# Feed-forward chunks by 512 weight columns, key-block products by 128 columns, 400 GB/s in the planner

## The chip, the core and the metric

The kernel runs on one NeuronCore of one Trainium2 chip. The metric is the device time of one execution in microseconds (us); lower is better.

## What is computed

Two layers on a sequence of 256 tokens of width 1024, batch 1. Each layer is feed-forward, attention, feed-forward. Every one of the six blocks is normalised and modulated by vectors that come from a conditioning vector `c`, and its result is added through a gate. The attention of layer 0 has 16 query and 4 key heads and a window of 128 tokens; that of layer 1 has 16 heads with forget gates.

```python
c_act = jax.nn.silu(c)
for layer in range(DEPTH):
    mod = (c_act @ ada_w[layer] + ada_b[layer]).reshape(B, 3, 3, D_MODEL)
    h = modulate(x, norm_g[layer, 0], mod[:, 0, 0], mod[:, 0, 1])
    x = x + 0.5 * mod[:, 0, 2][:, None, :] * swiglu(h, ffn_w13[layer, 0], ffn_w2[layer, 0])
    h = modulate(x, norm_g[layer, 1], mod[:, 1, 0], mod[:, 1, 1])
    y = swa_mixer(...) if layer == 0 else fox_mixer(...)
    x = x + mod[:, 1, 2][:, None, :] * y
    h = modulate(x, norm_g[layer, 2], mod[:, 2, 0], mod[:, 2, 1])
    x = x + 0.5 * mod[:, 2, 2][:, None, :] * swiglu(h, ffn_w13[layer, 1], ffn_w2[layer, 1])

def swiglu(h, w13, w2):
    gate, up = jnp.split(h @ w13, 2, axis=-1)
    return (jax.nn.silu(gate) * up) @ w2
```

The inner width of the feed-forward is 2816. All inputs are float32.

## The kernel before

**Precision.** Every large product is made of three. An operand is cut into a high part `hi` and a rest `lo` (`split`, `norm_T` and others: ACT casts, DVE subtracts), and `mm3` accumulates high times high, high times low, low times high. A weight tile of 128 x 1024 thus costs a transfer (`wraw`), a cast on ACT (`whi`) and a subtraction on DVE (`wlo`). The rows of the modulation matrix (`in_ada`) are multiplied on DVE by `dot`, in place in `wraw`.

**Feed-forward.** `ffn` goes through the inner width in 11 chunks of 256 gate and 256 up columns. A chunk needs four tiles of w13 and two of w2. There are two ways to compute a chunk. `chunk_b` holds 128 tokens of `hT` still and moves 512 weight columns (256 gate, 256 up): 24 matmuls for a half of the tokens, 48 for a chunk; the product is then natural (tokens in partitions), so that `finish_b` transposes it on PE, four 128-column transposes per chunk, and ACT and DVE cut the result into `gT`. `chunk_a` holds 128 weight columns still and moves all 256 tokens: 96 matmuls of 256 columns per chunk, and the product comes out transposed. Before, the first chunks of each feed-forward (four in the first, two in the others) go by `chunk_b`, the other 34 (7, 9, 9, 9) by `chunk_a`. `down` multiplies `gT` with w2: 24 matmuls of 512 columns per chunk and half.

**Attention.** `swa` (layer 0) and `fox` (layer 1) project per group of heads (`project`, 384 columns), normalise (`qk_norm`, with a power on POOL), and transpose. Per pair of heads `scores` makes 12 products, a softmax per head, and `values` transposes the probabilities (three blocks, tile `t`), cuts them into high and low (`PT`) and multiplies them with the values `vt`. There are two key blocks of 128. The second one is seen by the second 128 queries alone; before, its probabilities stand beside 128 columns of zeros, so that both blocks move 256 columns and add into the same 256 columns of `po`. Two tiles with such zeros are kept for the whole attention and used in turn (`PTs`); four more with zeros hold the values (`vts`). The trace calls all of them `zeroed`.

**Tiles.** Most tiles of 128 x 1024 come from one pool of 39 (`wp`): weights raw, high and low, `hT`, `gT`, `OT`, the masks, the values and the `PTs`.

**The planner.** The program is recorded first (`Recorder`). `run` then gives every instruction a due time, counted back from the place of the matmul that needs it, plays the program through with a cost per instruction, and so fixes the order on each engine; on the chip every engine works through its list in that order. A transfer counts in the due times with 1368 ns and its bytes at 343 GB/s, in the play with its bytes at 343 GB/s behind the transfer before it. For some instructions (the scaling of `t` by `den` among them) the play may choose ACT or DVE. All instructions are issued from line 238, so that the trace tells them apart by tiles alone.

Of the kernel before, what the change touches and what calls it, by code (L numbers as in the profile page):

```python
# [17 lines left out]
P = 128  # L18
# [18 lines left out]
BOTH = 1  # L37
AHEAD = (3, 3)
LAG = (3, 2)
NZ = (4, 2, 4, 2)  # L40
HOOK = (0, 0)
ALT = 800.0
EVAC = 8e3
# [135 lines left out]
class Recorder:  # L179
# [112 lines left out]
    def run(self, window=None):  # L292
# [14 lines left out]
        for o in reversed(ops):  # L307
            due = o.at if o.eng == "PE" else end
            for s in o.succ:
                due = min(due, s.due - o.dur - lat(o, s) - (DMARG + o.bytes / 343 if o.bytes else 0))  # L310
            if o.bg:
                due = min(due, o.at)
            if o.paced is not None:
                due = min(due, o.at)
            if o.eng != "PE" and any(b.psum for b in o.bases):
                due = min(due, o.at + EVAC)
            if o.urgent is not None:
                due = o.urgent
            o.due = due
# [61 lines left out]
        while len(done) < len(ops):  # L381
# [11 lines left out]
            for e in engines:  # L393
                while busy[e] <= t:
# [57 lines left out]
                        active += busy[e] - t  # L452
                    o.end = busy[e]
                    if o.bytes:
                        dma = max(dma, t + 1100) + max(o.bytes / 343, 60)
                        o.end = dma + 2000 * (e == "POOL")
                        busy[e] = t + 470
                        if e == "SP":
                            flight.append(dma + 910)
                            heapq.heappush(events, dma + 910)  # L460
# [20 lines left out]
def _build(ctx, rec, tc, nc, ap, out):  # L481
# [15 lines left out]
    def psum():  # L497
        return ps.tile([P, 512], F32, tag="ps", name="ps")
# [99 lines left out]
    def weights(name, n):  # L598
        pieces = plan[used[0] : used[0] + n]
        used[0] += n  # L600
        assert all(p[0] in name for p in pieces)
        return [split(load(p[1])) for p in pieces]

    def mm3(o, st, mv, start, stop):
        sh, sl = st
        mh, ml = mv
        T.matmul(o, sh, mh, start=start, stop=False)
        T.matmul(o, sh, ml, start=False, stop=False)
        T.matmul(o, sl, mh, start=False, stop=stop)
# [42 lines left out]
    def hTk(hT, k, tok):  # L652
        return hT[0][k // 4][:, k % 4, tok], hT[1][k // 4][:, k % 4, tok]
# [99 lines left out]
    def ffn(l, f, hT, pre, nT, hook, last, nb=2, tail=TAIL):  # L753
# [8 lines left out]
        def finish_b(g, h, gT):  # L762
            tok = slice(h * P, h * P + P)
            pt2 = psum()
            for ft in range(2):
                T.transpose(pt2[:, ft * P : ft * P + P], g[:, ft * P : ft * P + P], ident)
            pv = pt2[:, 0:256].rearrange("p (a b) -> p a b", a=2)
            A.copy(gT[:, 0, :, tok], pv)
            V.tensor_tensor(out=gT[:, 1, :, tok], in0=pv, in1=gT[:, 0, :, tok].bitcast(F32), op=ALU.subtract)
# [7 lines left out]
                mm3(pt, hTk(hT, k, tok), (hi[:, cc], lo[:, cc]), k == 0, k == KT - 1)  # L777
            return pt

        def chunk_a(w, gT, ft):  # L780
            pt = psum()
            for gu in range(2):
                for k in range(KT):
                    hi, lo = w[k // 2]
                    a = (k % 2) * 512 + gu * 256 + ft * P
                    mm3(pt[:, gu * 256 : gu * 256 + 256], (hi[:, a : a + P], lo[:, a : a + P]),
                        hTk(hT, k, slice(0, S)), k == 0, k == KT - 1)
            g = sp.tile([P, 256], F32, tag="s", name="sil")
            A.activation(g, pt[:, 0:256], AF.Silu)
            V.tensor_tensor(out=g, in0=g, in1=pt[:, 256:512], op=ALU.mult)  # L790
            A.copy(gT[:, 0, ft, :], g)
            V.tensor_tensor(out=gT[:, 1, ft, :], in0=g, in1=gT[:, 0, ft, :].bitcast(F32), op=ALU.subtract)

        accs = []

        def down(c, w, gT, halves, dhs=(0, 1)):
# [34 lines left out]
        for c in range(first, NCH):  # L831
            if c > first or not pre:
                w = w13(c)
            else:
                for q in pend:
                    q[1] = weights("w2", 2)
                w = w13(c)
            gT = gTs()
            if l + f == 0 and c == 6:
                small_inputs()  # L840
                swa_table()
            for ft in range(2):
                chunk_a(w, gT, ft)
                while late and (ft == 1 or len(late) > 2):
                    finish_b(*late.pop(0))
            pend.append([c, weights("w2", 2), gT])
            keep = max(1, tail - (NCH - 1 - c))
            while len(pend) > keep:
                down(*pend.pop(0), (0, 1))
        for h in range(2):  # L850
            for dhs in ((0,), (1,)) if last and h == 1 else ((0, 1),):
                for i, q in enumerate(pend):
                    if h == 1 and i == HOOK[0] and not last:
                        hook()
                    down(*q, (h,), dhs)
                yield h, accs[h], dhs


    PTs, vts = [], []

    def zeroed(nv, npt):

        vts.clear()
        PTs.clear()
        for n in range(max(nv, npt)):
            for tiles, m, na, c in ((vts, nv, 4, slice(HD, 2 * HD)), (PTs, npt, 2, slice(0, P))):
                if n < m:
                    t = wp.tile([P, W], F32R, tag="w", name="zeroed")
                    G.memset(t.bitcast(F32).rearrange("p (a c) -> p a c", a=na)[:, :, c], 0.0)
                    tiles.append(t)  # L870

    def qk_norm(pj, nqk):
        sq = bp.tile([P, 512], F32, tag="b", name="sq")
# [73 lines left out]
    def values(head, e, t, vt, po, OT):  # L947
        pT = pacc()

        for j, a in enumerate((257, 0, 129)):  # L950
            T.transpose(pT[:, j * P : j * P + P], t[:, a : a + P], ident)
        PT = PTs[head % len(PTs)].rearrange("p (a b) -> p a b", a=2)
        A.copy(PT[:, 0, 128:512], pT[:, 0:384])
        V.tensor_tensor(out=PT[:, 1, 128:512], in0=pT[:, 0:384], in1=PT[:, 0, 128:512].bitcast(F32), op=ALU.subtract)
        for kt in range(2):
            mv = slice(256, 512) if kt == 0 else slice(0, 256)
            vc = slice(e * HD, e * HD + P)
            mm3(po[:, 0:256], (vt[:, 0, kt, vc], vt[:, 1, kt, vc]), (PT[:, 0, mv], PT[:, 1, mv]),
                e == 0 and kt == 0, e == 1 and kt == 1)
        if e == 1:  # L960
            hp = head // 2
            if hp % 4 == 0:
                for i in range(2):
                    OT[i].append(wp.tile([P, 4, S], F32R, tag="w", name=f"OT{i}"))
            hi, lo = OT[0][hp // 4][:, hp % 4, :], OT[1][hp // 4][:, hp % 4, :]
            A.copy(hi, po[:, 0:256])
            V.tensor_tensor(out=lo, in0=po[:, 0:256], in1=hi.bitcast(F32), op=ALU.subtract)
# [79 lines left out]
    def swa(hT, nT):  # L1047
# [4 lines left out]
        def group(g):  # L1052
            w = weights("swin", 4)
            if g == 0:
                M.extend(swa_maps())
                zeroed(*NZ[:2])
            pq, pk = pacc(), pacc()
            a, b = (wp.tile([P, W], F32R, tag="w", name="qkv") for _ in range(2))
            part = lambda t, c: t[:, c : c + 512].rearrange("p (i s) -> p i s", i=2)
# [79 lines left out]
    def fox(hT, nT):  # L1139
# [5 lines left out]
        def group(j):  # L1145
            n = 400 if j == 0 else 384
            w = weights("fwin0" if j == 0 else "fwin", 4)
            if j == 0:
                zeroed(*NZ[2:])
            pq = pacc()  # L1150
            a = wp.tile([P, W], F32R, tag="w", name="qk")
            part = lambda c: a[:, c : c + 512].rearrange("p (i s) -> p i s", i=2)
# [127 lines left out]
```

## Time and profile before

| | us |
|---|---|
| three runs | 1002.23, 1003.95, 1004.24 |
| median | 1003.95 |
| profiled execution, its own time | 1004.72 |
| profiled execution, span from first to last instruction | 1002.9 |
| PE busy | 981.6 |
| DVE busy | 774.7 |
| ACT busy | 522.5 |
| POOL busy | 55.3 |

PE is the matrix engine, PEld its weight loads, DVE the vector engine, ACT the scalar engine, POOL GpSimd, SP the queue that issues the transfers. "Busy" is the time in which at least one instruction of the engine is shown; matmuls overlap, so that their spacing is read from the distance of their starts. A stage is a stretch of the span: first product 16 to 58 us, first feed-forward to 205, window attention to 305, second feed-forward to 500, third to 682, forget attention to 810, last feed-forward to the end.

### The profile page before, as it was taken

What the parts mean: (1) busy time and instruction counts of PE and PEld (TensorE: products, weight loads), DVE (VectorE), ACT (ScalarE), POOL (GpSimd) and SP (SyncE); (2) the same over time, 40 slices, a digit from 0 to 9 for tenths busy, and PEclk for the clock granted to TensorE, in tenths of its full rate; (3) what the DMA queues carried; (4) which work ended last, traced back from release to release, by engine and by line L of the source; (5) the groups of instructions that cost most, each with busy time, mean ns of one, the idle gap of its engine ahead of it and who ended that gap; (6) DMA issues with size and microseconds to landing.
All of it is one profiled execution on the core that took longest, in us unless ns stands there. A gap on an engine that the chain in (4) does not pass through costs nothing.

```text
span 1002.9 us, 16605 instructions
## 1 busy us (share of the span) xinstructions
PE 981.6 (98%) x6262; PEld 891.2 (89%) x6262; DVE 774.7 (77%) x1396; ACT 522.5 (52%) x946; POOL 55.3 (6%) x77
## 2 busy tenths in 40 slices
PE   6999999998999999999999999999999999999997
PEld 4898999897788899999889999989899789999996
DVE  5999788888999976677897767678788997555532
ACT  6473335465986543454544433447577675444420
POOL 1000000033000000000100000002211010000000
PEclk9999999999999999999999999999999999999999
DMA  9999899779446886786787878844536357656501
GB/s 344 409 354 399 332 391 308 253 269 294 148 150 253 330 316 225 318 302 237 283 315 275 311 274 306 317 157 153 166 128 249 137 191 263 212 191 240 189 33 64
DMA packets 74258, 252.92 MB, mean 252 GB/s; under 512 B 8497, under 2 KB 11969, under 8 KB 74178
## 3 DMA queue, kind: packets, MB, share of 16 engines
q1 hardware_dynamic: 73186, 249.63, 67.9%
q10 hardware_dynamic: 896, 2.21, 0.7%
q8 instruction: 49, 0.80, 0.3%
q0 software_dynamic: 96, 0.02, 0.1%
q14 instruction: 31, 0.25, 0.1%
HBM read 249.95 MB, written 1.88 MB: 251 GB/s over the span
## 4 chain that ended last, share of the span: by engine, by line
PE 91%; ACT 3%; DVE 3%; DMA 1%; POOL 1%; issue 1%; DVEq 0%; POOLq 0%
PE ps L238 57%; PE pa L238 33%; ACT t L238 1%; POOL qrs L238 1%; DVE wraw L238 1%; DMA sink<-in_sink 1%; DMA M<-foxsc 1%; DVE wlo L238 1%; ACT zeroed L238 0%; DVE qss L238 0%; DVE t L238 0%; ACT whi L238 0%; DVE qn L238 0%; ACT hT L238 0%; DVE qkv L238 0%
## 5 line engine op out<-in xcount | busy, mean ns | idle before, releaser
L238 DVE TENSOR_TENSOR wlo<-wraw,whi 128x1024 fp32r<-128x1024 f32 (+2 forms) x328 | 379.8, 1180 | 96.1 <-ACT whi L238 45.4
L238 ACT CAST whi<-wraw 128x1024 fp32r<-128x1024 f32 (+2 forms) x328 | 325.4, 1021 | 164.1 <-PE ps L238 74.5
L238 PE MATMUL ps<-hT,whi 128*128 128x256 f32 x2176 | 393.0, 283 | 0.0
L238 PEld LDWEIGHTS ps<-hT,whi 128*128 128x128 f32 x2176 | 341.0, 192 | 2.6 <-issue 0.6
L238 PE MATMUL ps<-hT,wlo 128*128 128x256 f32 x1088 | 307.7, 283 | 0.0
L238 PE MATMUL pa<-whi,gT 128*128 128x512 f32 x704 | 217.9, 391 | 0.3 <-DVE gT L238 0.3
L238 PEld LDWEIGHTS ps<-hT,wlo 128*128 128x128 f32 x1088 | 208.7, 192 | 0.0
L238 PE MATMUL ps<-whi,hT 128*128 128x384 f32 (+2 forms) x640 | 188.0, 365 | 1.4 <-DVE zeroed L238 1.4
L238 DVE SCALAR_TENSOR_TENSOR wraw<-wraw,cb 128x1024 f32<-128x1024 f32 x144 | 173.2, 1217 | 6.8 <-DMA wraw<-in_ada 6.8
L238 PEld LDWEIGHTS pa<-whi,gT 128*128 128x128 f32 x704 | 132.2, 188 | 27.7 <-DVE gT L238 0.7
L238 PE MATMUL pa<-wlo,gT 128*128 128x512 f32 x352 | 133.4, 391 | 0.0
L238 PEld LDWEIGHTS ps<-whi,hT 128*128 128x128 f32 x640 | 117.9, 189 | 12.8 <-DVE zeroed L238 1.8
L238 PE MATMUL ps<-wlo,hT 128*128 128x384 f32 (+2 forms) x320 | 116.6, 365 | 0.5 <-DVE wlo L238 0.5
L238 ACT ACTIVATE sil<-ps 128x256 f32<-128x256 f32 x84 | 31.8, 381 | 105.7 <-PE ps L238 105.7
L238 PEld LDWEIGHTS pa<-wlo,gT 128*128 128x128 f32 x352 | 66.1, 188 | 12.8
L238 PEld LDWEIGHTS ps<-wlo,hT 128*128 128x128 f32 x320 | 60.5, 189 | 6.5 <-DVE wlo L238 0.9
L238 DVE TENSOR_TENSOR sil<-sil,ps 128x256 f32<-128x256 f32 x84 | 34.6, 415 | 39.0 <-ACT sil L238 39.0
L238 ACT CAST gT<-sil 128x256 fp32r<-128x256 f32 x68 | 27.0, 405 | 61.1 <-DVE sil L238 54.2
L238 DVE TENSOR_TENSOR gT<-sil,gT 128x256 fp32r<-128x256 f32 x68 | 28.2, 421 | 18.8 <-ACT gT L238 18.8
L238 POOL TENSOR_TENSOR rs<-u,mhalf 128x1 f32<-128x1 f32 x12 | 14.5, 1209 | 484.5 <-DVE u L238 484.5
L238 PE MATMUL pa<-whi,OT 128*128 128x512 f32 x128 | 39.4, 392 | 0.0
L238 PE MATMUL pa<-zeroed 128*128 128x256 f32 x192 | 37.2, 300 | 2.2 <-ACT zeroed L238 1.8
(120 smaller groups left out, 732.2 us busy)
## 6 DMA issues: line engine op xcount, KB each, us to landing
wraw<-in_ada SPq DMA_DIRECT2D x144, 512.0 KB, 7.1
wraw<-in_w13b SPq DMA_DIRECT2D x132, 512.0 KB, 6.5
wraw<-in_w SPq DMA_DIRECT2D x88, 512.0 KB, 5.9
wraw<-in_w13a SPq DMA_DIRECT2D x28, 512.0 KB, 7.9
wraw<-in_fwin SPq DMA_DIRECT2D x28, 384.0 KB, 4.3
wraw<-in_w13s SPq DMA_DIRECT2D x16, 512.0 KB, 10.2
wraw<-in_swin SPq DMA_DIRECT2D x16, 384.0 KB, 7.2
wraw<-in_swout SPq DMA_DIRECT2D x8, 512.0 KB, 6.3
```

Of the source, the lines that this page charges most:

```text
L238: return lambda: getattr(real, method)(*[un(v) for v in a], **{n: un(v) for n, v in k.items()})
```

## The change

All chunks of all feed-forwards go by `chunk_b`; `chunk_a` is gone. The transposes of a chunk are issued behind the first half of the next one, those of the last chunk behind the loop. The second key block moves its own 128 columns and adds into the second 128 columns of `po` alone; `PT` is an ordinary tile of the pool, taken for each head, and needs no zeros; `zeroed` makes the four value tiles alone. The planner counts 400 GB/s in both places.

```diff
-NZ = (4, 2, 4, 2)
+NZ = 4
...
-                due = min(due, s.due - o.dur - lat(o, s) - (DMARG + o.bytes / 343 if o.bytes else 0))
+                due = min(due, s.due - o.dur - lat(o, s) - (DMARG + o.bytes / 400 if o.bytes else 0))
...
-                        dma = max(dma, t + 1100) + max(o.bytes / 343, 60)
+                        dma = max(dma, t + 1100) + max(o.bytes / 400, 60)
...
-            for ft in range(2):
-                chunk_a(w, gT, ft)
-                while late and (ft == 1 or len(late) > 2):
+            for h in range(2):
+                pt = chunk_b(w, h)
+                while late and h == 0:
                     finish_b(*late.pop(0))
+                late.append((gated(pt), h, gT))
             pend.append([c, weights("w2", 2), gT])
...
+        while late:
+            finish_b(*late.pop(0))
...
-        PT = PTs[head % len(PTs)].rearrange("p (a b) -> p a b", a=2)
-        A.copy(PT[:, 0, 128:512], pT[:, 0:384])
-        V.tensor_tensor(out=PT[:, 1, 128:512], in0=pT[:, 0:384], in1=PT[:, 0, 128:512].bitcast(F32), op=ALU.subtract)
+        PT = wp.tile([P, 2, 384], F32R, tag="w", name="PT")
+        A.copy(PT[:, 0, :], pT[:, 0:384])
+        V.tensor_tensor(out=PT[:, 1, :], in0=pT[:, 0:384], in1=PT[:, 0, :].bitcast(F32), op=ALU.subtract)
         for kt in range(2):
-            mv = slice(256, 512) if kt == 0 else slice(0, 256)
+            mv, tok = (slice(128, 384), slice(0, 256)) if kt == 0 else (slice(0, 128), slice(128, 256))
             vc = slice(e * HD, e * HD + P)
-            mm3(po[:, 0:256], (vt[:, 0, kt, vc], vt[:, 1, kt, vc]), (PT[:, 0, mv], PT[:, 1, mv]),
+            mm3(po[:, tok], (vt[:, 0, kt, vc], vt[:, 1, kt, vc]), (PT[:, 0, mv], PT[:, 1, mv]),
```

PE in the first feed-forward, before, at the end of a chunk: three matmuls of 256 columns (the two `hT` names are the high and the low part), repeated to 96 of them, and then the products with w2.

```order
L238 MATMUL ps<-hT_407,whi 128x256
L238 MATMUL ps<-hT_420,whi 128x256
L238 MATMUL ps<-hT_407,wlo 128x256
L238 MATMUL pa<-whi,gT 128x512
L238 MATMUL pa<-wlo,gT 128x512
L238 MATMUL pa<-whi,gT 128x512 x2
```

With the change, the middle of a chunk there: 24 matmuls of 512 columns end, four transposes of the chunk before follow, and the second half of the tokens begins.

```order
L238 MATMUL ps<-whi,hT_406 128x512
L238 MATMUL ps<-wlo,hT_406 128x512
L238 MATMUL ps<-whi,hT_419 128x512
L238 MATMUL ps<-ident,sil 128x128 x4
L238 MATMUL ps<-whi,hT_214 128x512
L238 MATMUL ps<-wlo,hT_214 128x512
L238 MATMUL ps<-whi,hT_226 128x512
```

The matmuls of a chunk go from 96 to 48, and PE gets four transposes per chunk between them.

DVE in the window attention, before, from the first scores on (`qn`, `kn`: normalised heads; `qkv`: transposed ones; `den`: the softmax sum; `wraw,mod`: a row of the modulation matrix; `wlo 128x768`: rest of a projection weight).

```order
L238 TENSOR_TENSOR qn<-ps,qrs 128x256
L238 TENSOR_SCALAR qss<-qss 128x5
L238 TENSOR_TENSOR wlo<-wraw,whi 128x768
L238 SCALAR_TENSOR_TENSOR qkv<-pa,qkg,qkv 128x256 x3
L238 TENSOR_TENSOR qn<-ps,qrs 128x256
L238 TENSOR_TENSOR wlo<-wraw,whi 128x768
L238 RECIPROCAL den<-den 128x2
L238 TENSOR_SCALAR t<-t,den 128x128
L238 TENSOR_TENSOR wlo<-wraw,whi 128x768
L238 SCALAR_TENSOR_TENSOR wraw,mod_2499<-wraw,cb 128x1024
L238 TENSOR_TENSOR zeroed<-pa,zeroed 128x384
L238 TENSOR_TENSOR wlo<-wraw,whi 128x768
```

DVE at the same place with the change.

```order
L238 TENSOR_TENSOR qn<-ps,qrs 128x256
L238 TENSOR_SCALAR kn<-ps,qrs 128x128
L238 TENSOR_TENSOR wlo<-wraw,whi 128x768
L238 RECIPROCAL den<-den 128x2
L238 TENSOR_SCALAR t<-t,den 128x256
L238 SCALAR_TENSOR_TENSOR wraw,mod_2083<-wraw,cb 128x1024
L238 TENSOR_TENSOR PT<-pa,PT 128x384
L238 SCALAR_TENSOR_TENSOR wraw,mod_2083<-wraw,cb 128x1024
L238 TENSOR_REDUCE qss<-sq 128x5
L238 TENSOR_SCALAR qss<-qss 128x5
```

Three of the four subtractions for projection weights behind the first scores now stand ahead of them, and the scaling by `den` stands on DVE where ACT had it. In the whole of the attention's softmax part (first exponential to last `OT`), ACT has 14 such scalings in place of 19 (the 128x256 form 6 in place of 11), DVE 18 in place of 13.

PE in the window attention, before, between two pairs of scores.

```order
L238 MATMUL pa<-zeroed 128x256 x7
L238 MATMUL pa<-ident,t 128x128 x3
L238 MATMUL pa<-zeroed 128x256 x6
L238 MATMUL ps<-qkv 128x128 x3
L238 MATMUL ps<-qkv 128x256 x3
```

With the change.

```order
L238 MATMUL pa<-ident,t 128x128 x3
L238 MATMUL pa<-PT,zeroed 128x256 x3
L238 MATMUL pa<-PT,zeroed 128x128 x3
L238 MATMUL pa<-ident,t 128x128 x3
L238 MATMUL pa<-PT,zeroed 128x256
```

Three of the six value products of a head have 128 columns in place of 256; nothing else is added there.

## Rows read from the trace of the kernel before

**Rows 1.** The page: busy time, chain of work by engine, the products of the gate.
```profile
PE 981.6 (98%) x6262; PEld 891.2 (89%) x6262; DVE 774.7 (77%) x1396; ACT 522.5 (52%) x946; POOL 55.3 (6%) x77
...
PE 91%; ACT 3%; DVE 3%; DMA 1%; POOL 1%; issue 1%; DVEq 0%; POOLq 0%
...
L238 ACT ACTIVATE sil<-ps 128x256 f32<-128x256 f32 x84 | 31.8, 381 | 105.7 <-PE ps L238 105.7
...
L238 DVE TENSOR_TENSOR sil<-sil,ps 128x256 f32<-128x256 f32 x84 | 34.6, 415 | 39.0 <-ACT sil L238 39.0
```
**Rows 2.** Busy time by stage; columns as in the first row.
```profile
core 0: us, PE busy (x) PEld busy (x) DVE busy (x) ACT busy (x) POOL busy (x), PEclk, DMA share, GB/s
16.00:58.00 42.00, 42.00 (x180) 34.57 (x181) 41.16 (x73) 19.62 (x28) 0.00 (x0) 1.00 1.03 409
58.00:212.00 154.00, 154.00 (x1020) 141.93 (x1019) 132.31 (x204) 74.84 (x120) 3.34 (x4) 1.00 0.88 327
232.00:252.00 20.00, 17.31 (x94) 14.65 (x93) 17.44 (x47) 10.71 (x26) 6.27 (x7) 0.91 0.83 271
252.00:276.50 24.50, 22.57 (x177) 18.85 (x176) 23.61 (x98) 23.97 (x89) 2.27 (x7) 1.00 0.41 148
717.00:772.00 55.00, 54.94 (x367) 52.21 (x368) 48.26 (x155) 42.95 (x114) 9.63 (x9) 1.00 0.47 165
```
**Rows 3.** The chain of work in order of time (start, us, what).
```profile
299.11 0.87 PE ps L238 x8
...
351.58 11.51 PE ps L238 x96
363.09 5.47 PE pa L238 x24
...
845.47 10.93 PE pa L238 x48
```
**Rows 4.** PE in order of time around four transposes of the third feed-forward.
```profile
528.43 0.60 PE L238 MATMUL ps<-ident,sil 128*128 128x128 f32 x4
528.78 0.48 PE L238 MATMUL pa<-whi,gT 128*128 128x512 f32 x1
529.10 0.40 PE L238 MATMUL pa<-wlo,gT 128*128 128x512 f32 x1
```
**Rows 5.** PE's groups by shape (busy us, mean ns).
```profile
L238 PE MATMUL pa<-zeroed 128*128 128x256 f32 x192 | 37.2, 300 | 2.2 <-ACT zeroed L238 1.8 <-DVE zeroed L238 0.2
...
L238 PE MATMUL ps<-qkv 64*128 64x256 f32 x48 | 7.0, 294 | 0.0
L238 PE MATMUL ps<-qkv 64*128 64x128 f32 x48 | 6.8, 289 | 0.0
```
**Rows 6.** The chain of work in the window attention.
```profile
227.65 0.86 DVE wlo L238
...
236.67 0.87 DVE wlo L238
...
252.71 1.15 DVE wraw L238 x2
253.97 1.68 ACT t L238 x6
...
269.47 1.96 ACT t L238 x8
```
**Rows 7.** ACT's and DVE's groups by shape: the scaling of the probabilities.
```profile
L238 ACT ACTIVATE t<-t,den 128x256 f32<-128x256 f32 x19 | 9.7, 511 | 1.4 <-DVE den L238 1.4
...
L238 DVE TENSOR_SCALAR t<-t,den 128x256 f32<-128x256 f32 x13 | 4.6, 351 | 0.2
```
**Rows 8.** ACT's waits.
```profile
ACT zeroed L238 <- PE pa L238: 2.2, 4, 1.0
```
**Rows 9.** Busy time in two stretches of ten us, columns as in rows 2.
```profile
16.00:26.00 10.00, 10.00 (x38) 8.10 (x39) 9.96 (x19) 5.39 (x9) 0.00 (x0) 1.00 1.03 410
...
106.00:116.00 10.00, 10.00 (x58) 8.13 (x58) 8.46 (x16) 2.95 (x5) 0.00 (x0) 1.00 0.92 331
```

More of the change, by code (lines that the diff above doesn't have):

```diff
@@ L778, in chunk_b @@
             return pt
[L780 to L792, printed above, removed]
         accs = []
@@ L856, in ffn, with zeroed @@
                 yield h, accs[h], dhs
-    PTs, vts = [], []
-    def zeroed(nv, npt):
+    vts = []
+    def zeroed(n):
         vts.clear()
[L864 to L870, printed above, removed]
+        for _ in range(n):
+            t = wp.tile([P, W], F32R, tag="w", name="zeroed")
+            G.memset(t.bitcast(F32).rearrange("p (a c) -> p a c", a=4)[:, :, HD : 2 * HD], 0.0)
+            vts.append(t)
     def qk_norm(pj, nqk):
@@ L1055, in group @@
                 M.extend(swa_maps())
-                zeroed(*NZ[:2])
+                zeroed(NZ)
             pq, pk = pacc(), pacc()
@@ L1148, in group @@
             if j == 0:
-                zeroed(*NZ[2:])
+                zeroed(NZ)
             pq = pacc()
```

## The prediction

> **What bounds the kernel now.** I read the page first, then the chain of work, then the busy time by stage. The page shows PE busy for 981.6 us, and the chain that ends last runs over PE for 91% of the span [rows 1]: what PE has to do, at the spacing of its matmuls, is nearly the whole time. By stage [rows 2] PE is busy without a break in the first product and the first feed-forward (42 of 42 us, 154 of 154) and all but unbroken in the forget attention (54.94 of 55); the other feed-forwards look the same. The window attention differs: from 252 to 276.5 us ACT is busy for 23.97 and DVE for 23.61 of 24.5 us, and the chain there runs over ACT's work on `t` and DVE's `wlo` and `wraw` [rows 6], PE waiting in between. So a feed-forward is priced by PE's spacing, the window attention by what ACT and DVE have to do.
>
> A change of 0.2% is about 2 us, which is what a measurement here can tell from nothing. The sum is made against the profiled execution's own time, 1004.72 us; the median of the three runs lies 0.8 us lower.
>
> **Feed-forward.** 34 chunks go from the one form to the other. The old form is 96 matmuls of 256 columns; one such run takes 11.51 us in the chain, 0.120 each [rows 3]. The new form is 48 of 512 columns; 48 such matmuls take 10.93 us and 24 take 5.47 us, 0.228 each [rows 3]. So 0.58 us per chunk goes, 34 x 0.58 = 19.7 us. Four transposes per chunk come. Eight of them take 0.87 us in the chain [rows 3], 0.109 each; and four of them between two streams of matmuls move the second next matmul from 528.43 to 529.10, which is 0.67 us with one matmul of 0.228 in it, 0.44 for the four [rows 4]. 136 x 0.109 = 14.8 us. Net: **-4.9 us**. I take both from PE's chain because nothing else has to be late for it: the two halves of ACT and DVE's work for a chunk keep their number and their 256 columns, so the load of both engines stays, and they have a chunk's time to do it.
>
> The transposes can make PE wait. In the middle of the program they stand behind a whole half chunk (5.47 us) that covers the gate's 0.381 us on ACT and 0.415 us on DVE [rows 1]. Only the last two transposes of a feed-forward stand close, five matmuls (1.14 us) behind the product they need; 0.80 us of it is ACT's and DVE's work, the rest is left for three handovers. I count nothing; between 0 and 0.5 us for each of four ends, 2 us at most, is the bound.
>
> **Value products.** 96 matmuls go from 256 to 128 columns. The trace of before has no 128-column product over all 128 rows in this precision. From above: it costs no more than the 256-column one, 0.120, for in the products of the scores the 128-column form is not shown longer than the 256-column one (289 against 294 ns, [rows 5]); saving nothing. From below: its time falls with its columns as it does from 512 to 256, which is 0.228 - 0.120 = 0.108 for 256 columns and 0.054 for 128; 96 x 0.054 = 5.2 us in all. I take 0.109, the spacing of the transposes [rows 3], which are the nearest row (128 columns, a new weight load each): 96 x 0.011 = 1.1 us. Half of them are in the window attention, where PE is not the bound; so **-0.5 us**, with ends of 0 and 2.6 for that half.
>
> The Trainium skill's page "TensorE: Matmul & The Clock Gate", section Back-to-back issue gap, puts a sustained 128-column matmul with its weight load at about 81 ns. By that the saving would be an estimated 0.039 each, 3.7 us in all and 1.9 in the half that counts. The same section gives 131 ns for 512 columns, where this trace shows 228, so I leave it beside the sum.
>
> **Tiles and POOL.** The four memsets for the zeros of `PT` go from POOL, which is busy for 55 us of 1003 [rows 1]: nothing. `PT` is now taken from the pool for each head. ACT now waits 2.2 us in four places until one of the two old tiles is free [rows 8]; that can go, but it may come back as a wait for a free tile (below).
>
> **The planner.** At 400 GB/s a tile of 512 KB counts 1.31 us where it counted 1.53. The chip moved 409 GB/s while the first product ran [rows 2], so the plan is nearer to what happens there. The order listing shows what follows. In the window attention three subtractions for projection weights and one row of the modulation move out of the softmax part, ahead of it; five 256-column scalings by `den` go from ACT to DVE. On ACT that takes away five instructions; six instructions of the kind sit at 1.68 us in the chain and eight at 1.96 [rows 6], a mean of 0.26 with short ones among them, and the 256-column scaling shows 0.511 busy [rows 7], of which I count 0.40: 5 x 0.40 = 2.0 us. On DVE it takes away 3 x 0.87 and, for a modulation row with its read of the sum (the x2 of the chain), 1.15 [rows 6], 3.8 us, and adds 5 x 0.35 = 1.8 [rows 7]: 2.0 us less too. Both engines are full there, so the stage should get shorter by that; I take **-2.0 us**. The ends: 0, if the handovers set the pace and not the load, and, with all the moved work (the four subtractions and two modulation rows that leave the whole stage from the first projection on, 4 x 0.87 + 2 x 1.15 = 5.8) off the path, -5.8.
>
> In the first product the six scalings that DVE made go to ACT. DVE is busy for 9.96 of 10 us there, ACT for 5.39 [rows 9], and PE shows no break: nothing, as PE sets the pace. If PE were freed there, it would be DVE that is late next.
>
> **Sum.** 4.9 + 0.5 + 2.0 = 7.4 us less: 1004.7 - 7.4 = 997.3. Against the median it would be 996.6; I say **997.0 us**.
>
> **Rivals.**
>
> *The attention gives nothing back.* The moved work is only work that waited anyway, and the transposes at the four ends cost a little: only the feed-forward's 4.9 us remain, 1004.7 - 4.9 = 999.8. For it speaks that handovers between three engines fill that stage; against it that two engines are 97% busy.
>
> *The attention gives all of it.* 4.9 + 0.5 + 5.8 = 11.2, 993.5 us. For it: the chain in that stage lies on exactly the instructions that move. Against it: something else ends last when they are gone, PE itself with 22.57 of 24.5 us busy first.
>
> *Transfers slower than planned.* The plan now relies on 400 GB/s. From 58 to 212 us the transfer engines were busy for 0.88 of the time at 327 GB/s [rows 2], and in one stretch 331 GB/s at 0.92 [rows 9], 360 if full. At that rate what is planned in 154 us takes 154 x 0.88 x (400 / 360 - 1) = 15 us longer; the idle 0.12 (18 us) can take all of it, but not where the loads bunch. Half of it on PE gives 997.0 + 7.5 = 1004.5: no change. The Trainium skill's page "DMA: Bandwidth & Descriptors", section Where 436 GB/s comes from, speaks for this rival: it says that transfers between HBM and SBUF are bound at about 358 GB/s by the memory's side. By that the trace differs: 410 GB/s over ten us [rows 9], and the measurement decides; I give the rival little.
>
> *Slower: `PT` waits for a tile of the pool.* Two tiles were kept for it; now each of 32 heads asks the same 39 tiles that hold the weights loaded ahead. ACT's list is fixed, so that a `PT` copy that waits holds every exponential behind it, in the stage where ACT is the bound. Priced by today's wait for a tile, 2.2 / 4 = 0.55 us [rows 8], on each of the 16 heads of the window attention: 8.8 us, and the 2.0 us of relief are not seen: 1004.7 - 5.4 + 8.8 = 1008. It costs more than the change brings from ten such waits on. Against it: the planner knows the 39 tiles and places `PT` only where one is free in its play.
>
> That the change does not do what it says is excluded by the order listing, which shows the 512-column chunks, the transposes and the 128-column products.
>
> **Numbers.** Forecast (997.0) 0.58; the attention gives nothing 0.17; gives all 0.10; transfers 0.05; `PT` waits 0.07; anything else, split between no change and slower, 0.03. Faster by over 0.2% are the first three: 0.85. Within 0.2%: transfers and some of the rest, 0.07. Slower: 0.08. The range holds the first three with the bounds of the ends and of the value products: from 993.5 less 2 for the value products, 991.5, to 999.8 plus 2 for the four ends, 1001.8.
>
> **What would show it.** In the profile of the changed kernel: runs of 24 matmuls at 5.47 us with four transposes between, 16.84 us per chunk with its w2 products in place of 16.98; no PE wait on `sil` in the middle of a feed-forward; value products of 128 columns spaced at 0.11; window attention 100 us long before, some 98 after. Wrong would be: a spacing of 512-column matmuls above 0.228 in the chunks; PE idle before `sil` transposes; ACT waiting for a tile before `PT`; PE breaks in the first feed-forward that end with a transfer.

## The result and the profile after

The changed kernel takes 995.38 us (median of four runs, 994.73 to 995.55) against 1004.1 us for the kernel before in the same session (1002.23 to 1004.57): a ratio of 0.9902 with an interval of 0.9873 to 0.993, 8.7 us less. Forecast were 7 us. Its profiled execution took 995.55 us and has a span of 993.8.

Instructions and busy times of the page of the changed kernel, to be held against [rows 1]:

```profile
span 993.8 us, 13650 instructions
...
PE 972.1 (98%) x4766; PEld 816.5 (82%) x4766; DVE 776.9 (78%) x1397; ACT 527.5 (53%) x945; POOL 50.6 (5%) x73
...
PE 92%; DVE 3%; ACT 2%; DMA 1%; issue 1%; POOL 0%; SPq 0%; DVEq 0%; POOLq 0%
```

PE is busy for 9.5 us less, about the 9.1 us by which the span fell, and the chain still runs over it. Where those 9.1 us come from is read from the starts of each stage's first matmul, in us:

| | to the first product | first product and first feed-forward | window attention | second | third feed-forward | forget attention | last feed-forward, end |
|---|---|---|---|---|---|---|---|
| before | 15.74 | 189.48 | 99.40 | 188.95 | 188.39 | 128.23 | 192.66 |
| after | 16.63 | 190.48 | 96.54 | 186.92 | 187.02 | 125.50 | 190.63 |
| difference | +0.9 | +1.0 | -2.9 | -2.0 | -1.4 | -2.7 | -2.0 |

The chain of the changed kernel in the second feed-forward (start, length, what):

```profile
349.40 11.37 PE ps L238 x52
360.77 5.44 PE pa L238 x24
...
467.78 1.39 PE pa L238 x6
469.17 0.22 PE ps L238 x2
469.38 16.15 PE pa L238 x71
```

A chunk is 48 matmuls and four transposes in 11.37 us, where 96 matmuls took 11.51 [rows 3]; with w2 it is 16.81 us. The last two transposes (469.17) follow their predecessor without a gap: the end of a feed-forward costs nothing.

The first feed-forward loses instead. The waits of PE there, 58 to 112 us (waited for: us, times, longest), and the chain before the longer one:

```profile
PE ps L238 <- DVE gT L238: 2.1, 2, 1.2
```

```profile
61.86 3.80 ACT whi L238 x4
65.66 0.04 issue
65.69 0.05 DVE wlo L238
65.74 1.08 issue
66.83 2.36 DVE wlo L238 x2
69.19 0.34 DVE gT L238
69.53 0.04 issue
69.57 6.08 PE ps L238 x26
```

The products of the first four chunks are computed ahead, and their sixteen transposes now stand together. PE stands still before the last two until DVE has read an earlier group out of its tile (`gT`); in DVE's list that instruction stands behind six `wlo` in a row, which keep it busy without a break from 62.3 to 69.2 us. The second wait, 0.9 us, comes at 108.5 us, again for a `gT` of DVE. The kernel before has twelve transposes at one place there and four later, and shows no such wait. PE in the changed kernel (start, length, what, idle time before and what ended it):

```profile
66.67 1.69 PE L238 MATMUL ps<-ident,sil 128*128 128x128 f32 x14
69.57 0.44 PE L238 MATMUL ps<-ident,sil 128*128 128x128 f32 x2 [1.21 <-DVE gT L238]
```

The stages as windows (PE, PEld, DVE, ACT, POOL busy with instructions, then granted clock, DMA share, GB/s), first before, then after: first product and feed-forward, window attention, forget attention.

```profile
15.70:205.20 189.50, 189.46 (x1155) 170.11 (x1156) 167.41 (x263) 91.07 (x137) 1.72 (x2) 1.00 0.94 354
205.20:304.60 99.40, 94.76 (x570) 82.93 (x569) 91.44 (x240) 73.64 (x190) 21.08 (x31) 0.98 0.63 212
682.00:810.20 128.20, 124.97 (x780) 113.99 (x779) 110.92 (x306) 90.61 (x223) 21.09 (x22) 1.00 0.50 175
```

```profile
16.60:207.10 190.50, 188.40 (x848) 154.70 (x848) 169.64 (x266) 98.83 (x146) 2.08 (x3) 1.00 0.93 356
207.10:303.60 96.50, 92.27 (x570) 81.75 (x569) 87.03 (x237) 70.68 (x184) 16.45 (x28) 0.96 0.61 209
677.60:803.10 125.50, 123.54 (x781) 113.46 (x780) 109.64 (x307) 89.02 (x220) 20.65 (x20) 1.00 0.53 178
```

In the window attention DVE has 4.4 us less to do and ACT 3.0; in the stage ahead of it they have 2.2 and 7.8 more. Work moved forward; the experiments below show that the gain of the one stage and the wait in the other come with it. The granted clock is worth a look: 0.96 in the window attention after, 0.98 before. The shorter stage had the lower clock.

### The profile page after: what moved, and what is told of

Read it like the earlier page. It is cut to its first block, busy times and chain, and to the rows that moved or that the text cites. A ratio compares the mean times of both kernels' runs of the same rounds, so it can differ in the third digit from the quotient of the medians.

```text
span 993.8 us, 13650 instructions
## 1 busy us (share of the span) xinstructions
PE 972.1 (98%) x4766; PEld 816.5 (82%) x4766; DVE 776.9 (78%) x1397; ACT 527.5 (53%) x945; POOL 50.6 (5%) x73
## 4 chain that ended last, share of the span: by engine, by line
PE 92%; DVE 3%; ACT 2%; DMA 1%; issue 1%; POOL 0%; SPq 0%; DVEq 0%; POOLq 0%
PE ps L238 59%; PE pa L238 34%; DMA wraw<-in_w13s 1%; DVE t L238 1%; ACT whi L238 1%; DMA M<-foxsc 1%; ACT t L238 0%; DVE PT L238 0%; DVE wlo L238 0%; POOL qrs L238 0%; DVE wraw L238 0%; ACT PT L238 0%; DVE qss L238 0%; SPq L238 0%; DVE qn L238 0%
## 5 line engine op out<-in xcount | busy, mean ns | idle before, releaser
L238 PE MATMUL ps<-whi,hT 128*128 128x512 f32 (+2 forms) x1728 | 534.5, 382 | 0.0
L238 PEld LDWEIGHTS ps<-whi,hT 128*128 128x128 f32 x1728 | 321.6, 188 | 53.5 <-issue 0.6
L238 PE MATMUL ps<-wlo,hT 128*128 128x512 f32 (+2 forms) x864 | 328.6, 381 | 0.0
L238 PEld LDWEIGHTS ps<-wlo,hT 128*128 128x128 f32 x864 | 162.5, 188 | 26.1 <-issue 0.2
L238 DVE TENSOR_TENSOR gT<-ps,gT 128x256 fp32r<-128x256 f32 x88 | 33.7, 418 | 9.0 <-ACT gT L238 8.9
L238 PE MATMUL pa<-PT,zeroed 128*128 128x256 f32 (+1 forms) x192 | 37.0, 297 | 0.4 <-ACT PT L238 0.4
L238 ACT CAST gT<-ps 128x256 fp32r<-128x256 f32 x88 | 29.2, 378 | 11.6 <-PE ps L238 10.9
L238 PEld LDWEIGHTS pa<-PT,zeroed 128*128 128x128 f32 x192 | 31.3, 203 | 2.7 <-DVE PT L238 0.7
L238 POOL TENSOR_TENSOR qrs<-qss,mhalf 128x4 f32<-128x4 f32 (+1 forms) x24 | 28.4, 1182 | 89.9 <-DVE qss L238 89.9
L238 ACT ACTIVATE t<-t,nm 128x129 f32<-128x129 f32 (+2 forms) x64 | 28.8, 452 | 2.9 <-DVE nm L238 2.8
## 6 DMA issues: line engine op xcount, KB each, us to landing
wraw<-in_w13a SPq DMA_DIRECT2D x28, 512.0 KB, 10.2
wraw<-in_w13s SPq DMA_DIRECT2D x16, 512.0 KB, 10.2
```

Source lines behind the costliest of these rows:

```text
L238: return lambda: getattr(real, method)(*[un(v) for v in a], **{n: un(v) for n, v in k.items()})
```

## The experiments

**Which part brings what.** The change has three parts: the feed-forward chunks, the value products (128 columns with a tile of the pool for each head), and 400 GB/s in the planner. The first session ran each alone, and the first two together.

The feed-forward part alone:

```diff
-            for ft in range(2):
-                chunk_a(w, gT, ft)
-                while late and (ft == 1 or len(late) > 2):
+            for h in range(2):
+                pt = chunk_b(w, h)
+                while late and h == 0:
                     finish_b(*late.pop(0))
+                late.append((gated(pt), h, gT))
```

> The feed-forward chunks alone (512 columns), the rest as before. Theory of the parts: PE's stream alone changes, 34 x 0.145 = 4.9 us less, of which the first feed-forward may give back some 2 us by transposes that wait, as it does in the changed kernel: 999 to 1001 us against 1004, the window attention still about 99.6 us long. Rival, the order: the attention changes by 2 us or more either way although nothing in it was edited, so anything from 997 to 1003.

Measured: 1000.83 us, ratio 0.9964 [0.9946, 0.9981]. The last three feed-forwards are 186.92, 187.02 and 190.65 us long, within 0.02 us of the whole change. The first is 187.78, and nearly all of the 1.7 us that it is under before lies in the first matmuls, not in the chunks (last section). With 343 GB/s the planner has put the sixteen transposes in two groups of eight, and PE waits for DVE 0.2 us there instead of 2.1:

```profile
61.42 1.03 PE L238 MATMUL ps<-ident,sil 128*128 128x128 f32 x8
66.21 1.03 PE L238 MATMUL ps<-ident,sil 128*128 128x128 f32 x8
```

The window attention is 100.71 us, 1.3 us longer than before: the order changed there too, though less than the rival asked for.

The value part alone:

```diff
-            mv = slice(256, 512) if kt == 0 else slice(0, 256)
+            mv, tok = (slice(128, 384), slice(0, 256)) if kt == 0 else (slice(0, 128), slice(128, 256))
```

> The value products alone (128 columns for the second key block, the PT tiles from the pool). Theory of the parts: 0.5 to 1 us less, 1003 to 1003.5. Rival, the value part makes the attention's gain (no wait for one of two kept tiles, fewer memsets): 3 to 5.5 us less, 998.5 to 1001, with both attentions about 3 us shorter. Rival, the pool: PT waits for a tile, slower than 1004.

Measured: 1001.91 us, 0.997 [0.9952, 0.9988], between the theory and the first rival. The execution that was profiled was the slowest of ten (1008.24 us), so its stages do not stand for the median: the forget attention is 127.54 us, the window attention 104.77, longer than before, at a mean granted clock of 0.92:

```profile
204.80:309.60 104.80, 99.86 (x571) 87.62 (x570) 91.39 (x244) 73.04 (x186) 20.27 (x29) 0.92 0.61 203
```

400 GB/s alone:

```diff
-... DMARG + o.bytes / 343 ...
+... DMARG + o.bytes / 400 ...
-                        dma = max(dma, t + 1100) + max(o.bytes / 343, 60)
+                        dma = max(dma, t + 1100) + max(o.bytes / 400, 60)
```

> The 400 GB/s alone. Theory of the parts: the window attention gets 2 to 3 us shorter since projection weights are split ahead of it, the first feed-forward keeps its length: 1001 to 1002. Rival, it is the other parts: 1004, no change. Rival, too optimistic a plan: PE waits in the first feed-forward, 1004 to 1007.

Measured: 1003.15 us, 0.9986 [0.9974, 0.9998], less than the theory expected. The window attention is 96.65 us, as expected, but the third feed-forward is 1.1 us longer than before.

The change without 400 GB/s:

> Feed-forward chunks and value products, transfers still counted at 343 GB/s (the change with its planner part undone). Theory of the parts: 995.4 plus the 2 to 3 us that the planner part brings, 997.5 to 998.5. Rival, the planner part brings nothing or costs the waits in the first feed-forward: 993 to 995.5.

Measured: 999.17 us, 0.9941 [0.9923, 0.9959], so that the rival falls; window attention 102.50 us, of which 10.2 at the lower clock. The two other pairs came in the second session.

Feed-forward part and 400 GB/s, value products as before:

> The change with the value products left as before: feed-forward chunks and 400 GB/s. Theory A, the parts add: the feed-forward part brought 0.36% and 400 GB/s 0.14%, so a ratio of 0.995, 999.5 us; window attention near 96.6 us, since it was 96.5 and 96.7 in both kernels with 400 GB/s so far. Theory B, the window attention is short because the second key block is narrower (fewer PE columns): the stage stays at 99 to 101 us and the kernel at that of the feed-forward part alone, 1000.8. Theory C, the order that comes out of the planner decides each time anew: the stage lies anywhere from 95 to 102 us. In every case the second to fourth feed-forwards lie 5.4 us under before, and the first feed-forward is 1 to 2 us longer than with the feed-forward part alone (187.8).

Measured: 996.84 us, 0.9932 [0.9904, 0.996], less than the 999.5 of theory A. The window attention is 94.67 us with 256 columns, so that theory B falls, and the granted clock is at its full level throughout:

```profile
206.80:301.50 94.70, 90.92 (x571) 80.26 (x570) 87.72 (x239) 69.48 (x182) 16.92 (x30) 1.00 0.60 211
```

Value part and 400 GB/s, chunks as before:

> The change with the feed-forward chunks left as before: value products of 128 columns and 400 GB/s. Theory A: 0.30% and 0.14% add, ratio 0.9956, 1000.1 us; window attention 96 to 97 us, forget attention 1 us under before, feed-forwards as before within 1 us. Theory B (value columns shorten the window attention): the same stage times, so this run does not separate B; with the run above it does. Theory C: window attention anywhere from 95 to 102 us.

Measured: 1002.0 us, 0.9972 [0.9952, 0.9991], more than theory A's 1000.1; in the profiled execution, the slowest of ten (1004.48 us), the window attention is 98.15 us, a little above what A expected, and the third feed-forward 0.9 us longer than before.

With these all eight combinations are there. With 0.9908 for the whole change (the mean of this ratio and that of its second measurement below), each part's effect is the mean over its four pairs, with and without it: feed-forward chunks -0.46%, value part -0.23%, 400 GB/s -0.19%, which are 4.6, 2.3 and 1.9 us, each uncertain by some 1.3 us by the intervals of the ratios. The sum is 8.8, about what the change brought. 400 GB/s brings 0.3% with the new chunks and 0.06% (a mean of -0.14 and +0.02) with the old ones, a difference hardly beyond its own uncertainty of 0.25%.

**What sets the window attention.** The stage was 94.7 to 104.8 us long in these profiles. Two things sort them: the planner's number, by what DVE has to do in the stage (91.4 to 94.6 us busy with 343, 86.9 to 88.0 with 400), and how long the granted clock stood at 0.50, that is 1.2 GHz. The changed kernel's windows around such a stretch:

```profile
247.00:249.00 2.00, 1.87 (x13) 1.49 (x12) 2.00 (x12) 0.99 (x4) 0.00 (x0) 1.00 0.46 178
249.00:254.20 5.20, 2.68 (x24) 1.90 (x23) 4.87 (x23) 4.63 (x17) 1.43 (x3) 1.00 0.85 289
254.20:261.00 6.80, 6.80 (x37) 6.13 (x37) 5.47 (x19) 6.28 (x20) 0.56 (x3) 0.50 0.46 166
261.00:264.00 3.00, 3.00 (x32) 2.56 (x33) 2.26 (x13) 2.62 (x10) 0.19 (x1) 0.99 0.01 3
```

PE waits for half of 249 to 254.2 us (2.68 of 5.20 busy), then the clock is at 0.50 for 6.8 us in which PE has no break, and it comes back. The chain says what that does:

```profile
253.14 0.41 ACT t L238
253.54 0.14 issue
253.68 3.81 PE pa L238 x18
257.49 1.58 PE ps L238 x8
259.07 2.51 PE pa L238 x13
261.58 0.93 PE ps L238 x12
262.51 0.47 DVE t L238
...
268.41 1.84 PE pa L238 x15
```

In a stage that ACT and DVE bound, PE at half clock becomes the bound: 18 matmuls take 3.81 us here, 15 take 1.84 at 268.41 us, at full clock. But a half idle PE does not always lose its clock: in the same stretch of the run that kept it (feed-forward part and 400 GB/s, 249 to 254.2) PE was busy for 2.83 of 5.20 us.

**Two variants of the change.** The first has two tiles kept for `PT`:

```diff
-        PT = wp.tile([P, 2, 384], F32R, tag="w", name="PT")
+        PT = PTs[head % 2]
```

> The change, with two tiles kept for PT for the whole attention, as before the change, but 128 columns for the second key block as in the change. It separates the tile of the pool from the columns. Theory A: the tile is not waited for in either form (ACT waits 2.2 us in all before PT in both), so no difference: 995.4 us, plus or minus 1. Rival: the pool tile lets ACT run ahead of PE by more than two heads and brings part of the window attention's 2.9 and the forget attention's 2.7 us; then this kernel is 1 to 4 us slower, 996.5 to 999.5, with ACT waiting for PE before PT for more than 2.2 us.

Measured: 999.68 us, 0.9942 [0.9914, 0.9969], about 4 us above the change, which ran in other sessions; the two intervals overlap. The waits of ACT (waited for: us, times, longest), in this kernel and in the change:

```profile
ACT PT L238 <- PE pa L238: 5.2, 10, 1.0
```

```profile
ACT PT L238 <- PE pa L238: 2.2, 7, 0.9
```

The traces are for the rival: the pool's tile, which the prediction feared, helps. In the forget attention, from each matmul's start to the next one's, the 96 value products take 13.0 us before, 11.8 in the change and 11.5 with kept tiles, while the 48 transposes of `t` take 6.3, 4.6 and 6.2: the columns shorten the products (the matmuls behind them take most of it back, see below), and the tile shortens the waits at the transposes. That stage is 126.95 us with kept tiles and 125.50 without; the window attention is 98.43, of which 10.2 at half clock. The clock seems to be much of the rest of the 4 us: by the mean granted clock of each execution, its ten had 12 us at half clock on the mean, the change's nine had 6.4, and a microsecond of it costs some 0.35 us (last section).

The second has the sixteen transposes of the first chunks spread, those of four products, eight, behind each half of the next chunk:

```diff
-        first = len(pre)
+        first = pre_n = len(pre)
...
-                while late and h == 0:
+                for _ in range(first if pre_n and c == first else len(late) * (h == 0)):
                     finish_b(*late.pop(0))
```

> The change, with the transposes of the first chunks of the first feed-forward spread: four behind each half chunk in place of all sixteen at once. Theory: the 1.2 us in which PE stands still near 69.6 us, before the last two of sixteen transposes, come from DVE, which has not yet cut the fourth product; spread out they wait for nothing and the first feed-forward is 1.2 us shorter, 189.3 us in place of 190.5, total about 994.2 us, ratio to before 0.989. Rival: DVE is the bound of that stretch (it also has the subtractions for w13 and the modulation rows), so that the wait only moves to a later place, and the first feed-forward stays at 190 to 191 us and the total at 995.4. Other stages change by the planner's order alone, a few tenths.

Measured: 992.85 us, 0.988 [0.9846, 0.9914]. Both waits are gone, not moved; the chain of this kernel at the same place, and its first window:

```profile
57.95 1.13 PE pa L238 x5
59.08 15.37 PE ps L238 x76
74.45 5.68 PE pa L238 x25
```

```profile
16.60:204.80 188.20, 188.20 (x848) 154.97 (x848) 169.60 (x266) 98.19 (x146) 2.08 (x3) 1.00 0.94 360
```

PE is busy for 188.20 of 188.20 us with the same 848 matmuls, and DVE and ACT carry the same load as in the change. So DVE was late for those tiles, not overloaded. All ten profiles with the new chunks agree: in the four with sixteen transposes at one place PE is idle for 2.1 us in this stage, in the six with two groups of eight (by the spread, or by the order that 343 GB/s gives) for at most 0.2.

**Side by side.** The last session ran the change, the spread version and two variants of it.

> The change as it is, once more, so that it stands in the same call as the three others. Expected: 995.4 us again, within 1 us; window attention 94 to 98 us. Over the ten profiles so far that stage fits 99.0 us, less 4.0 with 400 GB/s, plus 0.34 for every microsecond in which TensorE's granted clock in it is at the lower level of 1.2 GHz (0 to 17 us of them), with no residue over 0.7 us; so this profile should lie within 0.7 us of that line whatever its clock does. If the stage were set by the columns of the value products, the line would not hold.

Measured: 995.55 us, 0.9914 [0.9899, 0.9928]. Window attention 96.69 us with 6.8 at half clock; the line gives 97.3, so it holds.

> The change with the transposes of the first chunks spread, once more. Theory: 2.2 us under the change in the first feed-forward (188.3 against 190.5) and the same elsewhere, so 993.2 us if the change shows 995.4. Rival: the 2.5 us between the two in different calls were scatter, and the two lie within 1 us here.

Measured: 995.4 us, 0.9917 [0.9898, 0.9937]: level with the change, as the rival said. The first feed-forward is again 2.4 us shorter (188.94 against 191.32). The profiled execution lost that to the clock: 17.1 us at half clock in the window attention, a stage of 101.88 us. The six runs go from 992.39 to 999.32 us. Their mean granted clocks sort them: three at 0.997 took 992.39 to 994.80 us, three at 0.991 to 0.993 took 995.99 to 999.32. A gain of 2 us in one stage is real in the trace, and not shown in the time: no version is shown to beat the change.

The spread version with the old value products:

> The spread version with the value products as before the change (256 columns for both key blocks, two kept tiles with zeros). Theory A: the 128 columns bring nothing in the window attention, which other engines bound, and 48 x 0.010 = 0.5 us in the forget attention: 0.5 us slower than the spread version, 993.5 to 994. Theory B: the shorter products leave PE idler in the window attention and its clock lower for longer (in six profiles with 128 columns 6.8 to 17.1 us of it at 1.2 GHz, in four with 256 columns 0 to 3.4): then this version has under 4 us at 1.2 GHz there and a window attention 1 to 3 us shorter, and is 1 to 2 us faster in all, 991.5. Theory C: the 128 columns bring the 0.3% that they brought alone: 996.

Measured: 996.28 us, 0.9921 [0.9908, 0.9934]. B was right on its stage (3.4 us at half clock, window attention 96.76 us), though executions of one kernel differ as much (last section), and wrong in sum: the forget attention is 128.23 us where the spread version has 124.62 and 125.41. C gives the total, though the loss lies in one stage.

The spread version with 343 GB/s:

> The spread version with 343 GB/s in the planner, as before the change. Theory: the window attention is 4.0 us longer at the same clock (98 to 103 us, on the line 99.0 + 0.34 per microsecond at 1.2 GHz); the first product starts 0.9 us earlier and the first feed-forward is 188 to 189 us as in the spread version, since the loss there with 400 GB/s lay in the waits that are now gone; in all 3 us slower than the spread version, 996. Rival: 400 GB/s costs 1.5 us in the first feed-forward whatever the transposes do, then this version has 186.5 to 187 us there and is only 1 to 1.5 us slower, 994.5.

Measured: 998.31 us, 0.9948 [0.9935, 0.9961], 2.9 us above the spread version. Window attention 102.89 us with 10.2 at half clock; the line gives 102.5. The first feed-forward is 187.33 us, between the two theories; but the first matmuls of this profile run at full speed from the start, those of the spread version do not (last section). Without that the stage is 187.3 us here and 186.9 in the spread version, so that the rival falls by these profiles: 400 GB/s costs nothing there once the transposes are spread.

```profile
15.80:203.10 187.30, 187.27 (x848) 153.81 (x849) 165.90 (x261) 90.12 (x137) 1.45 (x2) 1.00 0.95 361
203.10:306.00 102.90, 97.02 (x571) 85.49 (x570) 94.14 (x248) 72.27 (x186) 19.63 (x29) 0.95 0.59 199
```

With 343, DVE keeps 94.14 us in the window attention and ACT has 8 us less ahead of it: the planner's number alone moves that work.

All fourteen profiles, in order of length (low: us at a granted clock of 0.50 in the window attention). Each is one execution; those of the value part alone (1008.24 us, median 1001.91), of values and 400 (1004.48, 1002.0), of the change again (997.7, 995.55) and of the spread version again (999.32, 995.4) are the slowest of their runs.

| kernel | GB/s | columns, second block | window attention | low | forget attention |
|---|---|---|---|---|---|
| feed-forward, 400 | 400 | 256 | 94.67 | 0 | 127.81 |
| change | 400 | 128 | 96.54 | 6.8 | 125.50 |
| 400 alone | 400 | 256 | 96.65 | 3.4 | 127.33 |
| change again | 400 | 128 | 96.69 | 6.8 | 126.98 |
| spread, old values | 400 | 256 | 96.76 | 3.4 | 128.23 |
| spread | 400 | 128 | 97.97 | 6.8 | 124.62 |
| values, 400 | 400 | 128 | 98.15 | 10.2 | 126.29 |
| kept tiles | 400 | 128 | 98.43 | 10.2 | 126.95 |
| before | 343 | 256 | 99.40 | 3.4 | 128.23 |
| feed-forward alone | 343 | 256 | 100.71 | 3.4 | 129.91 |
| spread again | 400 | 128 | 101.88 | 17.1 | 125.41 |
| feed-forward, values | 343 | 128 | 102.50 | 10.2 | 126.15 |
| spread, 343 | 343 | 128 | 102.89 | 10.2 | 125.61 |
| values alone | 343 | 128 | 104.77 | 17.1 | 127.54 |

A least-squares line through them: 98.8 us, less 3.9 with 400 GB/s, plus 0.37 for each microsecond at half clock; no profile is off by more than 0.85. A term for the columns comes to -0.8 and hardly betters the fit. In the forget attention, where only three profiles (change again, feed-forward alone, values alone) have 3.4 us at half clock, the same fit gives -2.2 us for the value part and -0.3, within its scatter of 0.5, for 400 GB/s.

## Why the prediction was right

The total and the sign were right, and the three parts came out as 4.6, 2.3 and 1.9 us where 4.9, 0.5 and 2.0 were forecast. That the total is within 1.7 us is partly luck: by stage, the start and the first feed-forward are 2.9 us above the forecast, the attentions and the other feed-forwards 4.6 below. Inside the parts:

- **Feed-forward, right in mechanism and nearly in size.** The 48 matmuls and four transposes come to 11.37 us, 0.14 less than the 96, as forecast (0.145). The last three feed-forwards gave 5.4 us for 27 chunks (forecast 3.9), the same to 0.2 us in every version with these chunks. By the starts of the matmuls 4.2 us of it are the chunks and their transposes; 0.7 is a wait before the w2 products at 343.4 us in the kernel before, which is gone, and 0.5 lies behind the last matmul.
- **That ACT and DVE "have a chunk's time to do it": the step that failed.** It was argued from the middle of the program. In the first feed-forward the transposes of four chunks meet at one place, in the order that the planner makes with 400 GB/s, and PE waits for DVE there and once more, 2.1 us in all: the idle time before `sil` transposes that the prediction named as a sign of being wrong. Neither the chunks with 343 (0.2 us) nor the spread transposes show that wait. The term was -1.0 us for these seven chunks; it measured +1.0 in the change and -1.2 in the first spread run. With what the slow first matmuls cost taken off on both sides (last section: 1.5 us before, 0.9 in the change) it is +1.6 in the change, twice, and -1.0 to -1.1 in both spread runs: without the waits the forecast holds.
- **The four ends** cost nothing, as counted.
- **Value products: the columns right, the tile left out.** I took 0.109 for a 128-column product from a run of transposes, 0.011 less than for 256 columns. The timeline of PE in the changed kernel's forget attention (start, length, what):

```profile
721.44 0.28 PE L238 MATMUL pa<-PT,zeroed 128*128 128x256 f32 x1
721.55 0.34 PE L238 MATMUL ps<-wlo,hT 128*128 128x384 f32 x1
721.73 0.28 PE L238 MATMUL pa<-PT,zeroed 128*128 128x256 f32 x1
...
722.77 0.22 PE L238 MATMUL pa<-PT,zeroed 128*128 128x128 f32 x1
722.82 0.39 PE L238 MATMUL ps<-wlo,hT 128*128 128x384 f32 x1
723.05 0.22 PE L238 MATMUL pa<-PT,zeroed 128*128 128x128 f32 x1
723.11 0.57 PE L238 MATMUL ps<-whi,hT 128*128 128x384 f32 x2
```

The next matmul starts 0.11 us behind a 256-column product and 0.05 to 0.06 behind a 128-column one. But that next one, of 384 columns, then takes 0.23 until its own successor where it took 0.18. Product and next matmul together take 0.286 us (median of 19 such pairs) against 0.293 (median of 13 in the same stage): 0.007 less, so the columns are worth no more than forecast. By groups, from the kernel before to the change, the value products of the forget attention save 1.2 us, the matmuls of the projections and of the output behind them lose 1.0, the transposes of `t` save 1.7, the scores 0.2, and a wait before the first transposes of `qn` is 0.6 shorter. Without that wait the stage is 2.1 us shorter in the change and 0.3 with kept tiles: by these profiles some 0.3 us is the columns and 1.9 the pool's tile, to which the sum gave nothing. On the line through all profiles the value part gives 2.2 us there. The Trainium skill's page "TensorE: Matmul & The Clock Gate", section Back-to-back issue gap, has 81 ns for this size; the trace has 0.05 to 0.06 us up to the next matmul and 0.113 with what that one loses (0.286 less 0.173, the spacing of 384 columns in a run).
- **The planner: right in place and cause, under-sized.** The work that moves out of the softmax part did shorten the stage, by 3.9 us at the same clock, between the 2.0 I took and the end of 5.8. I did not count where the work goes: 0.9 us at the start (0.6 on the mean of the nine profiles with 400 against the five with 343), where the chain now ends with an ACT cast ahead of the normalisation, and the 2.1 us of waits. Alone it nets 1.4 us.
- **The rivals.** That the attention gives nothing or all is between the two. Slower transfers fell: the first feed-forward moved 356 GB/s after and 354 before, and no PE wait ended with a transfer. The wait of `PT` for a pool tile fell, and to the other side: ACT waits longer with kept tiles (5.2 us against 2.2).

The 2.9 us of the window attention are then 3.9 from the planner, less 1.3 for 3.4 us more at half clock (3.4 x 0.37), the rest within the scatter of the line.

## What to carry to other kernels

Price a change of matmul shape by the spacing in a whole chunk of the trace, with the matmuls behind the changed ones, and ask separately at the one place where buffered work piles up whether the engines that feed it are on time; that place gave back 2 us of the 5. A number in a planner is worth what it moves: compare the busy time of each engine stage by stage, since what one stage loses another takes on. And look at the granted clock, and at where its record begins, before comparing two profiles of a stage.

## What was not expected of the hardware

- **One kernel, many clocks.** In the nine profiles with 128-column value products the window attention has 6.8 to 17.1 us at a granted clock of 0.50, in the five with 256 columns 0 to 3.4, as if the shorter products brought the low clock on. That is not shown. The mean granted clock of every execution is on record, and twice the share that is missing from 1 is an estimate of the time at half clock, since the records have 0.50 and 1.00 alone: over the whole span 9.0 us on the mean of 59 executions with 128 columns, 7.2 on that of 88 with 256. The kernel before alone has executions from 0.998 to 0.989, that is from 4 to 22 us. Among executions of the same kernel in the same session (147 in all) a microsecond at half clock goes with 0.35 us more time, as on the line of the window attention (0.37). What it costs is thus shown twice; why it falls in one execution and not in the next of the same kernel stays open.
- **Half speed where the record of the clock is empty.** The first 512-column matmuls of the changed kernel, at the start of the first product:

```profile
17.22 0.63 PE L238 MATMUL pa<-wlo,hT 128*128 128x512 f32 x1
17.65 0.63 PE L238 MATMUL pa<-whi,hT 128*128 128x512 f32 x1
18.07 0.63 PE L238 MATMUL pa<-wlo,hT 128*128 128x512 f32 x1
```

They start 0.43 us apart, against 0.228 later, though the views give a granted clock of 1.00 there. The trace's record of the clock has its first entry, 1.00, at 18.69 us, just where the spacing falls to 0.23; time without an entry is counted as 1.00. So it is in all fourteen profiles: in eleven the first entry comes at 18.5 to 21.1 us and the first products are slow until then, in three (the feed-forward part alone, the value part alone, the spread version with 343 GB/s) it comes at 14.0 to 14.7, ahead of the first product, and none is slow. The first twenty of these matmuls take 4.7 us in those three, 5.6 in the change, 6.2 before and up to 6.7 (the spread version again). That is up to 2.0 us between profiles of one stage, and the first feed-forwards can only be compared without it. All three early ones have 343 GB/s, three of five, and none of nine with 400; whether the order ahead of the first product decides it was not tried.
